# Attention 0: norm factors stored, spread and applied, and outputs stored, each one tile later than the operation it needs

## The chip, the cores and the metric

The kernel runs on one core of a Trainium2 chip. Its time is the device time of one execution in microseconds (us). Five engines of the core matter here: PE (TensorE, matrix products; PEld is its weight load), DVE (VectorE), ACT (ScalarE), POOL (GpSimd) and SP (SyncE, which here only issues transfers). Each engine takes its instructions in the order in which the program has them; an instruction that must wait holds up what stands behind it on the same engine.

## The reference

A two-layer encoder trunk over 1024 positions of width 1024, in 32-bit floats. Layer 0 mixes positions by differential attention with 8 heads, layer 1 by latent attention; each layer has a gate path, an output projection and a residual add. The part that the change touches is the end of a head of layer 0:

```python
def block(qb):
    sc = jnp.einsum('bqhcd,bkhcd->bhcqk', qb, k) * scale
    p = jax.nn.softmax(sc, axis=-1)
    p = p[:, :, 0] - lam * p[:, :, 1]
    return jnp.einsum('bhqk,bkhd->bqhd', p, v)

o = _from_blocks(lax.map(block, _to_blocks(q)))
o = _rmsnorm(o, subln_g) * (1.0 - lambda_init)      # norm over the 128 values of a head
o = o.reshape(b, s, DA_WIDTH) * jax.nn.silu(z)      # gate
return o @ w_out0
```

## The kernel before, in words

Matrix products are made in three passes of a reduced format: each operand is split into a high part (a cast on ACT, to a tile whose name ends in h) and a low part (a subtraction on DVE or POOL, name ending in l). So `woh`, `wol` are the two parts of a weight tile of the output projection, `oah`, `oal` those of an operand tile, and their subtraction is L1199 on both engines. L173 to L175 are the three passes.

Attention 0 runs from about 155 to 685 us. A head takes about 70 us: eight tiles of 128 queries, in two halves of 512. PE makes the scores (L866), DVE and ACT the softmax, PE transposes the probabilities (L395), ACT and DVE split them (`pth` L397, `ptl` L398), and PE multiplies by v. Between these, PE works on the projections of the next heads, for which weights are loaded (`wraw`, L197) and split (`wh` L218 on ACT, `wl` L219 on POOL), and the rotation of q and k (rope, L331 to L370) runs over ACT, SP and POOL: `rp_raw` is copied out, SP swaps its halves into `rp_sw`, POOL multiplies and adds (L336, L341, L343), ACT casts to `qa`, POOL makes the low part `qb` (L366, L367), and SP moves both into place (L369, L370). L1102 to L1123 and L1133 to L1149 combine tiles of the weights and of the outputs for the projection, on POOL, with loads and stores on SP.

At the end of a half, `head_out` brings the output tile `o` out (ACT, L932) with its squares, and `subln` multiplies it by the gate tile `gz` (POOL, L938). The function `rest`, one tile later, sums the squares on PE and gets the norm factors `rq_y` on POOL (L169, L953). These are 512 numbers, 4 in each partition; to multiply `o` with them, each partition needs all 512. So they are stored to memory (`bc_d`, L420) and loaded back spread over all partitions (`bc_s`, L422). Then POOL multiplies (L908), and SP stores the tile to `oF` (L912), where the output projection loads it from. The very last half, (7,1), does not go through memory: its factors are spread by PE (L922).

The order is set so: a list `hooks` holds functions; at the end of each tile's work `after_scores` takes what is in the list at that point and runs it, so that a function which is put into the list by another runs one tile later. `in_turn` keeps the order in which the program is written for POOL, ACT and DVE instructions of this stage; the rest is set by a scheduler by the same writing order. In the last head `rest` is run from a list `rests` by the output projection's own steps (`extra0`), which also load tiles of `oF`: `k11`, `k21`, `k12` and four tiles `ob`. `k12` is the half (7,0); it is loaded right after attention 0 has ended (L1385), and split for the projection.

Of the kernel before, what the change touches and what calls it, by code (L numbers as in the profile page):

```python
# [11 lines left out]
F32 = mybir.dt.float32  # L12
# [9 lines left out]
P = 128  # L22
# [4 lines left out]
HF = 512  # L27
NH = 8
# [48 lines left out]
def f32v(ap):  # L77
    return ap.bitcast(F32)
# [3 lines left out]
def trunk(ctx: ExitStack, tc: tile.TileContext, A, out):  # L82
    nc = tc.nc
    SP, PE, V, S, G = nc.sync, nc.tensor, nc.vector, nc.scalar, nc.gpsimd

    def pool(stack, name, bufs=1, side="left", space=None):
        kw = dict(name=name, bufs=bufs, reuse_waits="tile")
        if space is not None:
            kw["space"] = space
            if space == DRAM:  # L90
                kw.pop("reuse_waits")
        else:
            kw["side"] = side
        return stack.enter_context(tc.tile_pool(**kw))
# [21 lines left out]
    def bank(tag, name, shape=None):  # L116
        nonlocal turn
        if tag == "acc":
            turn += 1
            if (turn - 1) % (2 + NB.get("accx", 0)) < 2:  # L120
                return psa.tile([P, HF], F32, name=name, tag="acc", bufs=2)
            tag = "accx"
        return ps.tile(shape or [P, HF], F32, name=name, tag=tag, bufs=NB[tag])

    dr = pool(ctx, "dr", bufs=1, space=DRAM)
# [6 lines left out]
    oF = [dr.tile([NH, 2, P, HF], F32, name=f"oF{l}") for l in range(2)]  # L132
# [47 lines left out]
    def behind(eng):  # L180

        return tc.issue_after(mk[eng]) if eng in mk else nullcontext()

    def in_turn(ins):

        return tc.keep_in_program_order(ins) if mk else ins
# [230 lines left out]
    def bcast_rows(sp, y, tag, bufs):  # L417

        d_ = dr.tile([HF], F32, name="bc_d", tag="bcd", bufs=4)
        SP.dma_start(d_.rearrange("(p t) -> p t", p=P), y)  # L420
        b = sp.tile([P, HF], F32, name="bc_s", tag=tag, bufs=bufs)
        SP.dma_start(b, d_[None, :].to_broadcast([P, HF]))  # L422
        return b, b.rearrange("p (q t) -> p t q", t=4)

    def t3(ap_):
        return ap_.rearrange("p (t q) -> p t q", t=4)
# [173 lines left out]
    for f in range(2):  # L600
        fs = slice(f * HF, f * HF + HF)
        spread = PE.matmul(cb[:, fs], ones[0:1, :], crow[0:1, fs], start=True, stop=True).ins
# [298 lines left out]

    def finish(o, y, l, h, half, dst, ap_, dgs):

        if dst is None:
            b, rb = bcast_rows(ap_, y, "osq", 4)

            def scale():
                in_turn(G.tensor_mul(t3(o), t3(o), rb))  # L908
                hooks.append(lambda: hooks.append(store))

            def store():
                SP.dma_start(oF[l][h, half], o)  # L912

            if l == 0 and (h, half) >= (NH - 2, 1):
                hooks.append(lambda: hooks.append(scale))
            else:
                hooks.append(scale)
            return
        rb = bank("z", "rb") if l else Y[1]
        for j in range(4):  # L920
            js = slice(j * P, (j + 1) * P)
            S.mul(dgs[:, js], ident, y[:, j : j + 1])  # L922
            PE.matmul(rb[:, js], ones, dgs[:, js], start=True, stop=True)
        V.tensor_mul(o, o, rb)
# [9 lines left out]
    def subln(o, sq, zz, half, h, dst):  # L934


        if dst is None:
            in_turn(G.tensor_mul(o, o, GZ[h][half]))  # L938
        else:
            V.tensor_mul(o, o, GZ[h][half])  # L940

        def rest():
            pt = Y[0] if dst is not None else ssq_at[0] if ssq_at else bank("acc", "ssq")
            for j in range(4):
                PE.matmul(pt[:, j : j + 1], sq[:, j * P : (j + 1) * P], ones[:, 0:1], start=True, stop=True)
            w = sm.tile([P, 4], F32, name="sl_w")
            fin = sm.tile([P, 4], F32, name="sl_f")
            V.tensor_mul(fin, zz, zz)
            V.scalar_tensor_tensor(out=w, in0=fin, scalar=P * EPS / GUARD ** 2, in1=pt[:, 0:4], op0=ALU.mult, op1=ALU.add)
            V.scalar_tensor_tensor(out=fin, in0=fin, scalar=FMAX / GUARD ** 2, in1=w, op0=ALU.mult, op1=ALU.is_ge)  # L950
            V.tensor_scalar(w, w, 3.0e38, None, op0=ALU.min)
            y = rsqrt(w, 4)
            in_turn(G.tensor_mul(y, y, fin))  # L953
            if dst is not None:
                return lambda: finish(o, y, 0, h, half, dst, None, sq)
            finish(o, y, 0, h, half, None, a0b, sq)

        if dst is None:
            (hooks if h < NH - 1 else rests).append(rest)
        else:  # L960
            return rest()
# [29 lines left out]
    tails, hooks = [None, None], []  # L991
# [171 lines left out]
    class Seven:  # L1163
# [32 lines left out]
        def put(self, raw, hi, lo, eng):  # L1196
            with behind("S"):
                S.copy(hi, raw)  # L1198
            sub = eng.tensor_sub(lo, raw, f32v(hi))  # L1199
            if eng is G:  # L1200
                in_turn(sub)
                self.sub = sub.ins
# [871 lines left out]
    def attn1(h, fills, extra=None, late=None):  # L2074
# [5 lines left out]
        def close(half, o_, zz):  # L2080
            if late and half == 1:
                ctx_["late"] = late(o_, zz, ctx_["gz"])
                return
            o = ap2.tile([P, HF], F32, name="o1", tag="o", bufs=2)
            V.scalar_tensor_tensor(out=o, in0=o_, scalar=0.5, in1=ctx_["gz"], op0=ALU.mult, op1=ALU.mult)
            V.reciprocal(zz, zz)
            finish(o, zz, 1, h, half, None, ap2, None)
# [365 lines left out]
```

## Time and profile before

| | us |
|---|---|
| median of the runs (3) | 1396.46 |
| lowest, highest | 1396.01, 1397.87 |
| profiled execution | 1394.95 |
| its span | 1393.2 |
| granted clock of TensorE, mean | 0.999 |
| PE busy | 1367.5 (98%) |
| DVE busy | 928.3 (67%) |
| POOL busy | 753.1 (54%) |
| ACT busy | 740.9 (53%) |

The span is the time from the first to the last instruction that the profile records; all times of instructions are counted from its start. Busy shares are means over the whole span. In rows of the timeline stand start, duration, engine, line, operation, output and inputs, shapes and count, and in brackets the idle time of the engine just before with what ended it. Of the 15 multiplications L908 the first is at 204.74 and the last at 674.75 us.

### The profile page before, as it was taken

How to read it: one execution, taken by the hardware profiler on the slowest of the kernel's cores; microseconds unless marked ns; L12 is line 12 of the kernel's file. 1: busy time of each engine (PE TensorE's matmuls, PEld its weight loads, DVE VectorE, ACT ScalarE, POOL GpSimd, SP SyncE). 2: the span in 40 equal slices, each digit the busy share in tenths (PEclk: the TensorE clock that was granted, in tenths of full speed). 3: DMA queues.
4: the chain of work that ended last, by engine and by line, in shares of the span. 5: the costliest groups of instructions: out<-in, count | busy, mean ns of one | idle time of the engine just before them, and what ended most of it. 6: DMA issues, size and time to landing. Idle time of an engine off the chain costs nothing.

```text
span 1393.2 us, 20695 instructions
## 1 busy us (share of the span) xinstructions
PE 1367.5 (98%) x7334; PEld 1144.7 (82%) x7334; DVE 928.3 (67%) x1313; ACT 740.9 (53%) x1339; POOL 753.1 (54%) x593
## 2 busy tenths in 40 slices
PE   9999999999999999999999999999999999999997
PEld 6788888888888887887887888888888888888886
DVE  7655777777666666668596976545656555555684
ACT  5532465656565555567648553335454544545554
POOL 5424374758686858575794233532141373834673
PEclk9999999999999999999999999999999999999999
DMA  9857644343444434526564246489443364667463
GB/s 342 263 177 244 201 110 141 100 144 105 149 127 144 128 121 122 151 61 212 182 219 167 68 137 212 137 282 286 125 105 119 102 201 136 193 221 215 145 245 121
DMA packets 149386, 232.06 MB, mean 167 GB/s; under 512 B 20641, under 2 KB 57633, under 8 KB 149282
## 3 DMA queue, kind: packets, MB, share of 16 engines
q1 hardware_dynamic: 149282, 230.74, 52.7%
q8 instruction: 58, 0.95, 0.3%
q14 instruction: 46, 0.38, 0.1%
HBM read 144.74 MB, written 61.81 MB: 148 GB/s over the span
## 4 chain that ended last, share of the span: by engine, by line
PE 79%; DVE 6%; DMA 5%; ACT 3%; POOL 3%; issue 2%; SPq 1%; POOLq 0%; ACTq 0%; DVEq 0%
PE s L2067 10%; PE acc L173 9%; PE acc L175 9%; PE acc L174 9%; PE tr L395 7%; PE s L866 7%; PE pv L173 4%; PE pv L174 4%; PE pv L175 4%; PE vps L173 2%; PE vps L174 1%; PE vps L175 1%; PE zacc L175 1%; PE zacc L173 1%; PE zacc L174 1%
## 5 line engine op out<-in xcount | busy, mean ns | idle before, releaser
L397 ACT CAST pth<-tr 128x512 fp32r<-128x512 f32 x256 | 150.3, 587 | 285.7 <-PE tr L395 280.8
L412 DVE TENSOR_REDUCE nm<-s 128x1 f32<-128x1024 f32 x192 | 233.8, 1218 | 79.8 <-PE s L866 70.9
L398 DVE TENSOR_TENSOR ptl<-tr,pth 128x512 fp32r<-128x512 f32 x256 | 176.1, 688 | 150.3 <-ACT pth L397 146.3
L219 POOL TENSOR_TENSOR wl<-wraw,wh 128x512 fp32r<-128x512 f32 (+2 forms) x77 | 98.8, 1284 | 208.4 <-ACT wh L218 176.3
L414 ACT ACTIVATE e<-s,nm 128x1024 f32<-128x1024 f32 x128 | 143.5, 1121 | 35.4 <-DVE nm L412 35.0
L395 PE MATMUL tr<-ident,e 128*128 128x128 f32 x1024 | 155.0, 273 | 4.1 <-DVE ptl L398 3.8
L395 PEld LDWEIGHTS tr<-ident,e 128*128 128x128 f32 x1024 | 120.7, 140 | 46.5 <-DVE ptl L398 24.1
L173 PE MATMUL acc<-h0h,wh 128*128 128x512 f32 x360 | 150.2, 417 | 0.0
L173 PE MATMUL pv<-pth,vt 128*128 128x256 f32 x512 | 147.5, 288 | 0.0
L174 PE MATMUL pv<-ptl,vt 128*128 128x256 f32 x512 | 145.6, 284 | 0.0
L175 PE MATMUL pv<-pth,vt 128*128 128x256 f32 x512 | 144.6, 282 | 0.0
L175 PE MATMUL acc<-h0h,wl 128*128 128x512 f32 x360 | 141.5, 393 | 0.0
L174 PE MATMUL acc<-h0l,wh 128*128 128x512 f32 x360 | 141.1, 392 | 0.0
L336 POOL TENSOR_TENSOR rp_r<-rp_raw,cosT 128x512 f32<-128x512 f32 x36 | 47.0, 1305 | 104.4 <-ACT rp_raw L333 52.9
L173 PEld LDWEIGHTS pv<-pth,vt 128*128 128x128 f32 x512 | 97.2, 190 | 2.9 <-ACT pth L397 0.2
L174 PEld LDWEIGHTS pv<-ptl,vt 128*128 128x128 f32 x512 | 97.4, 190 | 2.4
L175 PEld LDWEIGHTS pv<-pth,vt 128*128 128x128 f32 x512 | 97.3, 190 | 0.0
L1199 POOL TENSOR_TENSOR wol<-wol,woh 128x512 fp32r<-128x512 f32 x56 | 82.3, 1492 | 26.0 <-ACT woh L1198 24.4
L866 PE MATMUL s<-ks,qa 128*128 128x512 f32 x256 | 82.7, 403 | 4.4 <-DVE e L874 3.2
L874 DVE SCALAR_TENSOR_TENSOR e<-s,z,e 128x1024 f32<-128x1024 f32 x64 | 82.2, 1284 | 2.2
L866 PE MATMUL s<-ks,qb 128*128 128x512 f32 x256 | 79.8, 393 | 1.2 <-DMA qb<-qb 1.2
L175 PEld LDWEIGHTS acc<-h0h,wl 128*128 128x128 f32 x360 | 67.6, 188 | 15.1
(427 smaller groups left out, 3461.1 us busy)
## 6 DMA issues: line engine op xcount, KB each, us to landing
ada<-in_ada_ss SPq DMA_DIRECT2D x32, 512.0 KB, 5.9
wraw<-in_w_s SPq DMA_DIRECT2D x64, 256.0 KB, 2.8
vS<-v_hl SPq DMA_DIRECT2D x32, 512.0 KB, 5.9
vt<-vS SPq DMA_DIRECT2D x32, 512.0 KB, 4.9
wol<-tS SPq DMA_DIRECT2D x56, 256.0 KB, 5.2
tS<-ob SPq DMA_DIRECT2D x48, 256.0 KB, 2.0
rp_sw<-rp_raw SPq DMA_DIRECT2D x160, 64.0 KB, 2.0
bc_s<-bc_d SPq DMA_DIRECT2D x34, 256.0 KB, 4.2
```

Of the source, the lines that this page charges most:

```text
L173: PE.matmul(psum, ah, bh, start=first, stop=False, skip_group_check=skip)
L174: PE.matmul(psum, ah, bl, start=False, stop=False, skip_group_check=skip)
L175: mm3.last = PE.matmul(psum, al, bh, start=False, stop=last, skip_group_check=skip).ins
L219: sub = (V if pair_of else G).tensor_sub(l_[:, :n], raw[:, :n], f32v(h_[:, :n]))
L395: transpose_p.last = PE.transpose(tr[:, j, :], p[:, kt * P : (kt + 1) * P], ident).ins
L397: mk["S"] = S.copy(pth[kh][:, :, dst], tr).ins
L398: mk["V"] = V.tensor_sub(ptl[kh][:, :, dst], tr, f32v(pth[kh][:, :, dst])).ins
L412: mk["V"] = V.reduce_max(nm, s_ps, axis=AX.X, negate=True).ins
L414: mk["S"] = S.activation(e, s_ps, AF.Exp, bias=nm, scale=1.0, accum_out=zs).ins
L866: PE.matmul(s_ps[:, kc * HF : (kc + 1) * HF], src[:, c, ql], KS[h][kc][:, c, :], start=fst, stop=not fst)
L1199: sub = eng.tensor_sub(lo, raw, f32v(hi))
L2067: PE.matmul(s_ps[:, kc * HF : (kc + 1) * HF], lhs, rhs(kc), start=i == 0, stop=i == 4)
```

## The change

For layer 0, `finish` becomes a chain of four hooks. Before, the factors were stored and loaded back at once where they had been made, the multiplication ran one tile later (two for the halves (6,1) and (7,0)), and the store of the output two tiles after it. Now each of store of factors, spread load, multiplication and store of the output is a hook put into the list by the one before: one, two, three and four tiles after the factors. Layer 1 keeps its order. No instruction is added or removed; lines behind `finish` have numbers higher by 20, so L1199 is L1219, L938 is L958, and L908, L912, L420, L422 are L919, L923, L909, L914 for layer 0.

```diff
     def finish(o, y, l, h, half, dst, ap_, dgs):
 
+        if dst is None and l == 0:
+            d_ = dr.tile([HF], F32, name="bc_d", tag="bcd", bufs=4)
+            rb = []
+
+            def put():
+                SP.dma_start(d_.rearrange("(p t) -> p t", p=P), y)
+                hooks.append(spread)
+
+            def spread():
+                b = ap_.tile([P, HF], F32, name="bc_s", tag="osq", bufs=4)
+                SP.dma_start(b, d_[None, :].to_broadcast([P, HF]))
+                rb.append(b.rearrange("p (q t) -> p t q", t=4))
+                hooks.append(scale)
+
+            def scale():
+                in_turn(G.tensor_mul(t3(o), t3(o), rb[0]))
+                hooks.append(store)
+
+            def store():
+                SP.dma_start(oF[l][h, half], o)
+
+            hooks.append(put)
+            return
         if dst is None:
             b, rb = bcast_rows(ap_, y, "osq", 4)
...
-            if l == 0 and (h, half) >= (NH - 2, 1):
-                hooks.append(lambda: hooks.append(scale))
-            else:
-                hooks.append(scale)
+            hooks.append(scale)
             return
```

Where this moves instructions is shown at three places. The first is POOL in head 4: the multiplication of the half (3,1) by its factors, and the gate of the half (4,0). Before:

```order
L343 TENSOR_TENSOR rp_r<-rp_r,rp_sw 128x512
L219 TENSOR_TENSOR wl<-wraw,wh 128x512
L908 TENSOR_TENSOR o<-o,bc_s 128x512
L1112 TENSOR_TENSOR ob_4305<-ob_4305,c_202 128x512 x2
L358 TENSOR_TENSOR ks<-rp_r,ks 64x512
L359 TENSOR_TENSOR ks<-rp_r,ks 64x512
L336 TENSOR_TENSOR rp_r<-rp_raw,cosT 128x512
L341 TENSOR_TENSOR rp_sw<-rp_sw,sinT 128x512
```

Ten rows of POOL later, and in the changed kernel at the same place:

```order
L336 TENSOR_TENSOR rp_r<-rp_raw,cosT 128x512
L358 TENSOR_TENSOR ks<-rp_r,ks 64x512
L359 TENSOR_TENSOR ks<-rp_r,ks 64x512
L219 TENSOR_TENSOR wl<-wraw,wh 128x512
L958 TENSOR_TENSOR o<-o,gz 128x512
L919 TENSOR_TENSOR o<-o,bc_s 128x512
L1142 TENSOR_TENSOR ob_4303<-ot_4670,ob_4303 128x512
L1143 TENSOR_TENSOR ob_4304<-ob_4304,ot_4670 128x512
L341 TENSOR_TENSOR rp_sw<-rp_sw,sinT 128x512
L343 TENSOR_TENSOR rp_r<-rp_r,rp_sw 128x512
```

The multiplication by the factors has moved from behind a weight split to right behind the gate of the next half; the rest of the order is the same. It is the same move for the other halves before (7,0).

The second place is POOL at the end of attention 0: the multiplication of the half (7,0), the splits for the output projection, the split of the tile `k` that is loaded from this half's store, and the factors of the last half. Before:

```order
L1199 TENSOR_TENSOR wol<-wol,woh 128x512
L908 TENSOR_TENSOR o<-o,bc_s 128x512
L1199 TENSOR_TENSOR oal<-oal,oah 128x512
L1199 TENSOR_TENSOR wol<-wol,woh 128x512 x2
L1199 TENSOR_TENSOR oal<-k_6673,oah 128x512
L1145 TENSOR_TENSOR ob<-ob 128x512
L1146 TENSOR_TENSOR ob<-ob 128x512
L1148 TENSOR_TENSOR ob<-ob 128x512
L1149 TENSOR_TENSOR ob<-ob 128x512
L169 TENSOR_TENSOR rq_y<-sl_w,mhalf 128x4
```

And in the changed kernel:

```order
L1219 TENSOR_TENSOR wol<-wol,woh 128x512
L1219 TENSOR_TENSOR oal<-oal,oah 128x512
L1219 TENSOR_TENSOR wol<-wol,woh 128x512 x2
L919 TENSOR_TENSOR o<-o,bc_s 128x512
L1219 TENSOR_TENSOR oal<-k_6670,oah 128x512
L1165 TENSOR_TENSOR ob<-ob 128x512
L1166 TENSOR_TENSOR ob<-ob 128x512
L1168 TENSOR_TENSOR ob<-ob 128x512
L1169 TENSOR_TENSOR ob<-ob 128x512
L169 TENSOR_TENSOR rq_y<-sl_w,mhalf 128x4
```

The multiplication has moved behind three splits and stands directly ahead of the split of `k`, its own product loaded back.

The third place is SP's queue there (`tS`, `sS` and `oF` are in memory; a load of `k` or `ob` reads stored outputs). Before:

```order
L1355 DMA ob<-oF_81 128x512 x4
L1179 DMA wol<-tS_83 128x512
L1179 DMA oal<-oF_81 128x512
L1179 DMA wol<-tS_83 128x512
L1179 DMA oal<-oF_81 128x512
L420 DMA bc_d<-rq_y 128x4
L422 DMA bc_s<-bc_d 128x512
L1179 DMA wol<-tS_83 128x512
L1179 DMA oal<-oF_81 128x512
L1179 DMA wol<-tS_83 128x512
L912 DMA oF_81<-o 128x512
L1385 DMA k_6673<-oF_81 128x512
```

And in the changed kernel:

```order
L1199 DMA wol<-tS_83 128x512
L923 DMA oF_81<-o 128x512
L909 DMA bc_d<-rq_y 128x4
L1372 DMA k_6669<-oF_81 128x512
L1375 DMA ob<-oF_81 128x512 x4
L914 DMA bc_s<-bc_d 128x512
L923 DMA oF_81<-o 128x512
L1405 DMA k_6670<-oF_81 128x512
L1199 DMA wol<-tS_83 128x512 x4
L1199 DMA oal<-sS_85 128x512 x2
```

All loads of `wol` and `oal` that stood between now stand ahead, the store of the half (6,1) and the loads of `ob` come behind them, and the spread load of the last factors stands directly ahead of the store that it leads to.

## The prediction

> **What bounds the kernel now.** I read the page's head first, then the waits of PE by the stage that the change touches (140 to 700 us), then the engines' own timelines there.
>
> ```profile
> span 1393.2 us, 20695 instructions
> PE 1367.5 (98%) x7334; PEld 1144.7 (82%) x7334; DVE 928.3 (67%) x1313; ACT 740.9 (53%) x1339; POOL 753.1 (54%) x593
> PE s L866 <- DVE e L874: 3.2, 6, 1.0
> PE tr L395 <- DVE ptl L398: 2.8, 5, 0.9
> ```
>
> PE is busy 1367.5 of 1393.2 us, so all its idle time is 25.7 us. In attention 0 the largest idle groups (sum, count, longest) are 3.2 and 2.8 us. The change adds and removes no instruction, so the time moves only where one of PE's waits vanishes, grows or appears. I therefore follow each moved operation until a PE instruction waits for what stands behind it, or until an idle gap absorbs it.
>
> What moves is small. For each of 15 output tiles (head, half), one multiplication by the spread norm factors (L908, about 1.55 us on POOL) moves later in POOL's order, and three transfers move later in SP's. In the new order each L908 stands right behind the gate multiplication L938 of the next half. Both queues run in order; the outputs stay the same tiles and sizes, so no transfer gets longer by itself. Whatever stood behind the old place can run earlier by up to 1.55 us plus any wait for the factors, and what stands behind the new place runs 1.55 us later, unless idle time there takes it.
>
> **The change, part by part.** In heads 0 to 2 POOL has idle time between either place and its next consumer, and PE's few waits there are for other things; I cost them at nothing. Heads 3 to 6 are tighter.
>
> Head 3 gains:
>
> ```profile
> 376.25 1.55 POOL L908 TENSOR_TENSOR o<-o,bc_s 128x512 f32<-128x512 f32 x1 [1.83 <-DMA bc_s<-bc_d]
> 386.35 1.29 POOL L341 TENSOR_TENSOR rp_sw<-rp_sw,sinT 128x512 f32<-128x512 f32 x1 [1.95 <-DMA rp_sw<-rp_raw]
> 391.87 0.69 ACT L932 ACTIVATE o<-pv,g 128x512 f32<-128x512 f32 x1
> 396.81 1.29 POOL L938 TENSOR_TENSOR o<-o,gz 128x512 f32<-128x512 f32 x1
> 403.27 1.29 POOL L219 TENSOR_TENSOR wl<-wraw,wh 128x512 fp32r<-128x512 f32 x1
> 409.96 0.70 PE L866 MATMUL s<-ks,qa 128*128 128x512 f32 x2 [0.88 <-DMA qa<-qa]
> 411.22 0.70 PE L866 MATMUL s<-ks,qb 128*128 128x512 f32 x2 [0.55 <-DMA qb<-qb]
> ```
>
> Each row is start, duration, engine, line, operands and, in brackets, the idle time ahead with what ended it. The old L908 cost 1.83 idle plus 1.55 busy, up to 3.4 us, and the swap transfer of rope behind it is issued earlier, so the 1.95 at 386.35 need not return. L938 can go at 392.56 + the queue, about 393.4 (o is ready at 391.87 + 0.69), against 396.81: 3.4 earlier. The moved L908 then takes 1.55 back: 1.85 net at L219 (403.27), whose input buffer the next weight load of SP waits for, with the qa and qb copies queued behind it. PE's two waits are 0.88 and 0.55, both under 1.85, so both go: **-1.4**.
>
> Heads 4 and 6 lose:
>
> ```profile
> 446.39 1.54 POOL L908 TENSOR_TENSOR o<-o,bc_s 128x512 f32<-128x512 f32 x1
> 450.99 2.41 SPq L335 DMA_DIRECT2D rp_sw<-rp_raw  x4
> 454.95 1.29 POOL L341 TENSOR_TENSOR rp_sw<-rp_sw,sinT 128x512 f32<-128x512 f32 x1 [0.43 <-DMA rp_sw<-rp_raw]
> 465.53 1.30 POOL L938 TENSOR_TENSOR o<-o,gz 128x512 f32<-128x512 f32 x1
> 471.96 0.62 ACT L364 CAST qa<-rp_r 64x512 fp32r<-64x512 f32 x1 [2.23 <-POOL rp_r L343]
> 475.10 0.66 PE L395 MATMUL tr<-ident,e 128*128 128x128 f32 x4 [0.87 <-DVE ptl L398]
> 603.24 1.28 POOL L938 TENSOR_TENSOR o<-o,gz 128x512 f32<-128x512 f32 x1 [4.07 <-ACT o L932]
> 612.51 0.62 ACT L364 CAST qa<-rp_r 64x512 fp32r<-64x512 f32 x1 [2.28 <-POOL rp_r L343]
> 615.16 0.66 PE L395 MATMUL tr<-ident,e 128*128 128x128 f32 x4 [0.40 <-DVE ptl L398]
> ```
>
> In head 4 the old L908 (446.39) goes, but L341 at 454.95 still waits for a transfer that SP issues at 450.99, so its 1.54 us come back as idle. From 454.95 POOL runs without a gap through L938 at 465.53, and the L908 put behind that makes rope's last step 1.55 later. ACT waits for that step already (2.23), in order, ahead of the probability splits that PE waits for at 475.10 (0.87 now). Nothing between has slack, so the wait grows by the whole: **+1.5**. Head 6 is the same: L938 at 603.24 has 4.07 idle before it, so nothing done earlier helps, and ACT's 2.28 and PE's 0.40 each grow by 1.55: **+1.5**. In head 5 ACT also waits for rope, by
>
> ```profile
> 541.99 0.62 ACT L364 CAST qa<-rp_r 64x512 fp32r<-64x512 f32 x1 [1.60 <-POOL rp_r L343]
> 551.32 0.70 PE L866 MATMUL s<-ks,qb 128*128 128x512 f32 x2 [0.66 <-DMA qb<-qb]
> ```
>
> and its cast comes later by between nothing and 1.55, by how much of the time that the old L908 frees survives until then (POOL has no gap in between, but its inputs come from SP and ACT at their own times); I take 0.95, past the middle towards the late end, as head 4 gave back nothing; but the spread load, which was issued ahead of the qb copies that PE waits 0.66 for, now stands behind them. I set the two against each other: **0**, with ends -0.7 and +1.0.
>
> The junction with the output projection carries the largest term. The half (7,0) is stored and loaded back as an operand (k) of that projection:
>
> ```profile
> 674.75 1.57 POOL L908 TENSOR_TENSOR o<-o,bc_s 128x512 f32<-128x512 f32 x1
> 677.51 2.53 POOL L1199 TENSOR_TENSOR wol<-wol,woh 128x512 fp32r<-128x512 f32 x2
> 677.18 0.64 ACT L1198 CAST woh<-wol 128x512 fp32r<-128x512 f32 x1
> 682.06 1.29 POOL L1199 TENSOR_TENSOR oal<-k,oah 128x512 fp32r<-128x512 f32 x1 [2.02 <-ACT oah L1198]
> 683.31 1.29 POOL L1145 TENSOR_TENSOR ob<-ob 128x512 f32<-128x512 f32 x1
> 687.41 1.60 POOL L1149 TENSOR_TENSOR ob<-ob 128x512 f32<-128x512 f32 x1
> 689.32 1.02 POOL L169 TENSOR_TENSOR rq_y<-sl_w,mhalf 128x4 f32<-128x4 f32 x1 [0.30 <-DVE sl_w L951]
> 676.34 0.32 SPq L912 DMA_DIRECT2D oF<-o  x1
> 678.40 0.32 SPq L1385 DMA_DIRECT2D k<-oF  x1
> 678.77 1.85 SPq L1179 DMA_DIRECT2D wol<-tS  x4
> k<-oF SPq DMA_DIRECT2D x1, 256.0 KB, 2.7
> 690.65 1.28 ACT L922 ACTIVATE sq<-ident,rq_y 128x128 f32<-128x128 f32 x4 [4.42 <-POOL rq_y L953]
> ```
>
> L908 moves from 674.75 to behind three L1199 splits. The last two took 2.53 together from 677.51; with L908 out of their way all three come 1.5 earlier, except that the last can't start before ACT's cast of its operand ends (677.18 + 0.64 = 677.82). It ends at 679.1 (half of 2.53 later), so L908 runs from 679.1 to 680.65, 4.35 later than before. Then, step by step: the store is issued at 680.7; the load 2.06 later (678.40 less 676.34), at 682.7; it lands 2.7 later, at 685.5; cast to 686.1; the split oal<-k at 686.15 against 682.06; the four multiplications L1145 to L1149, queued behind it, take 5.7 and end at 693.1; then rq_y, the norm factor of the last half, against 689.32. It is 3.8 late. ACT's scaling, which already waits 4.42 for it, and then DVE follow:
>
> ```profile
> 692.48 1.29 DVE L1199 TENSOR_TENSOR oal<-oal,oah 128x512 fp32r<-128x512 f32 x2 [3.23 <-ACT oah L1198]
> 693.69 0.68 DVE L1199 TENSOR_TENSOR oal<-ob,oah 128x512 fp32r<-128x512 f32 x1
> 695.50 0.69 DVE L1420 TENSOR_TENSOR x<-x,oz 128x512 f32<-128x512 f32 x1 [0.53 <-PE oz L175]
> 707.86 1.78 DVE L1199 TENSOR_TENSOR oal<-ob,oah 128x512 fp32r<-128x512 f32 x1
> 710.00:720.00 10.00, 10.00 (x45) 8.26 (x44) 10.00 (x11) 3.89 (x8) 10.00 (x7) 1.00 0.35 127
> 726.90 0.50 PE L173 MATMUL oz<-woh,oah 128*128 128x512 f32 x1 [0.37 <-DVE x L1420]
> ```
>
> DVE's run starts at 692.48, has one gap of 0.53 (695.50) and then none: the window row gives, from the third number, busy time of PE, PEld, DVE, ACT and POOL, and DVE and POOL are busy all ten us. So 3.8 - 0.5 = 3.3 stay in it until PE waits for it at 726.90, with 0.37 of idle already, that is with no slack left. **+3.3**. Its ends: 0 if PE's wait is really set by something not delayed (PE could then run ahead), and 4.35 if the 0.53 gap does not absorb.
>
> Here a rule speaks against my 3.3. The row first: the same DVE subtraction took 0.68 at 693.69, when POOL was idle, and 1.78 at 707.86 beside a busy POOL. The Trainium skill, "SBUF — State Buffer", section "Who interferes with whom", says that a DVE instruction with two SBUF inputs and a GpSimd instruction that reads SBUF exclude each other, one fully blocking the other. These two rows agree. By that rule the shift of 3.8 on POOL against 3.3 on DVE changes which operations meet, by 0.5 us, which could free or hit one subtraction: 1.1 either way, so the sum would be 3.8 or 6.0 instead of 4.9.
>
> On SP four loads of wol stand behind the load of k; they were issued from 678.77 and now go from about 683.1. At the 2.7 that k took, or even twice that, they land by 690, ahead of DVE's and POOL's work on them, which starts after rq_y: 0, and up to +1 if the transfers bunch. One queue thing helps: the operand loads that stood behind (7,0)'s factor store on SP now stand ahead of it.
>
> Elsewhere SP's stores and loads issued later only find more room: in heads 0 to 2 the transfers they pass have no PE wait behind them. In head 7 before the junction POOL's idle time for the factors of (6,1) goes, but the casts on ACT, whose order hardly changes, set what follows: 0, at best -0.5.
>
> **The sum**: -1.4 + 1.5 + 0 + 1.5 + 3.3 = +4.9. The profiled execution took 1394.95 us (span 1393.2 and 1.75 around it), 1.51 under the median of the runs shown. Against it: 1399.85; on the median, 1396.46 + 4.9 = **1401.4**.
>
> **Rivals.**
> - *The junction absorbs.* PE's wait at 726.90 is only 0.37, and a PE that waits for DVE there might be given the time back at the end of the projection, or the split oal<-k may be overtaken in effect by faster transfers (SP's queue is emptier). Then only -1.4 + 1.5 + 1.5 = +1.6 stays: 1398.1. For it: PE has other idle time in the projection. Against it: DVE and POOL both full in 710 to 720.
> - *Larger loss.* The gain in head 3 fails, because L938 is held by POOL work that depends on other transfers, and the same late step costs its 1.55 there: +4.9 + 1.4 + 1.5 = +7.8; with head 5's +1.0 it is 1405.2. Against it: the 1.83 of idle at 376.25 is plainly lost to the spread load.
> - *Faster.* Taking transfers that POOL waits for out of its way is all that matters, and L908 finds cover wherever it stands. This is decided in the junction: from the point where k's split is ready by 682.06 after all, nothing is late. Then PE's waits 0.88, 0.55 and 0.66 go and head 7 gives 0.5 to 0.8: -2.8, 1393.6. Against it: the wait of 2.02 at 682.06 shows that k is already the last to arrive before the L908 moves 4.35 later.
> - *The change does nothing measurable*: the reordering is real in heads 4 and 6, but every cost is absorbed: 1396.5. It lies in the first rival's side of the range.
>
> **How the numbers follow.** The likeliest is the sum, 1401.4, with 0.56; its own range is 1399.3 to 1403.5 (the rule's 1.1, and one of the 1.5 terms out). The junction absorbed or all absorbed: 0.27. Larger loss: 0.10. Faster: 0.07. A measurement of this kernel tells about 0.2% (2.8 us) from no change: 1393.7 to 1399.3 counts as same. So slower is 0.56 + 0.10 = 0.66, same 0.27, faster 0.07. The range of 8 in 10 leaves out the faster case and the far end of the large loss, and takes in absorption: 1396.0 to 1405.0.
>
> **What would show it.** In the changed kernel: PE's waits at 410 for qa and qb gone; the waits of transposes for DVE's ptl near 475 and 615 above 1.5; the (7,0) scale near 679, the split of k near 686, rq_y near 693, DVE's run from about 696; PE idle in 699 to 735 of some 3 us more in all. The forecast is wrong if k lands before 683, if DVE's run shows gaps in 700 to 735, or if POOL has idle time between the moved L908 and rope in heads 4 and 6.

## The result and the profile after

The changed kernel takes 1404.2 us (median of 6 runs, 1403.39 to 1404.7) against 1396.36 (6 runs, 1394.79 to 1397.87) of the kernel before: a ratio of 1.0055, 95% interval [1.0042, 1.0068], so 5.9 to 9.5 us slower. The forecast was 1401.4 with 1396.0 to 1405.0: the direction and the range hold, and the loss of 7.8 us is 1.6 times the 4.9 forecast. The profiled execution has a span of 1401.5 us.

The head of its page, and the largest groups of PE's waits in the same window as before (sum, count, longest):

```profile
span 1401.5 us, 20683 instructions
PE 1369.4 (98%) x7334; PEld 1144.2 (82%) x7334; DVE 931.9 (66%) x1313; ACT 741.1 (53%) x1339; POOL 757.5 (54%) x593
PE s L866 <- DVE e L874: 4.8, 5, 1.2
PE tr L395 <- DVE ptl L398: 4.7, 7, 1.1
PE oy L175 <- POOL oal L1219: 1.1, 2, 0.6
PE oy L173 <- ACT oah L1218: 1.1, 1, 1.1
PE oy L174 <- POOL wol L1219: 1.0, 1, 1.0
```

PE's busy time hardly moved (1367.5 to 1369.4); what grew is waiting. The two groups that led before grew by 1.6 and 1.9, three at the junction are new or larger, and the waits for the copies of qa and qb near 410 are gone. The places, in the timelines of the changed kernel, head 3 first:

```profile
393.76 1.30 POOL L958 TENSOR_TENSOR o<-o,gz 128x512 f32<-128x512 f32 x1
395.02 1.56 POOL L919 TENSOR_TENSOR o<-o,bc_s 128x512 f32<-128x512 f32 x1
471.98 0.62 ACT L364 CAST qa<-rp_r 64x512 fp32r<-64x512 f32 x1 [3.78 <-POOL rp_r L343]
472.18 0.74 PE L866 MATMUL s<-ks,qa 128*128 128x512 f32 x2 [1.15 <-DVE e L874]
475.12 0.66 PE L395 MATMUL tr<-ident,e 128*128 128x128 f32 x4 [1.05 <-DVE ptl L398]
483.44 1.30 POOL L341 TENSOR_TENSOR rp_sw<-rp_sw,sinT 128x512 f32<-128x512 f32 x1 [5.03 <-DMA rp_sw<-rp_raw]
544.80 0.62 ACT L364 CAST qa<-rp_r 64x512 fp32r<-64x512 f32 x1 [2.58 <-POOL rp_r L343]
547.94 0.66 PE L395 MATMUL tr<-ident,e 128*128 128x128 f32 x4 [0.89 <-DVE ptl L398]
615.59 0.62 ACT L364 CAST qa<-rp_r 64x512 fp32r<-64x512 f32 x1 [3.78 <-POOL rp_r L343]
615.77 0.74 PE L866 MATMUL s<-ks,qa 128*128 128x512 f32 x2 [1.15 <-DVE e L874]
626.40 1.29 POOL L341 TENSOR_TENSOR rp_sw<-rp_sw,sinT 128x512 f32<-128x512 f32 x1 [4.38 <-DMA rp_sw<-rp_raw]
```

Head 3's gate comes at 393.76 (396.81 before). ACT's wait for rope in heads 4 and 6 grew from 2.23 and 2.28 to 3.78, by the 1.5 of the moved multiplication, and PE waits twice for what comes after: 1.15 for DVE's `e`, where it had no wait before, and then 1.05 (head 4) and 0.57 (head 6, at 618.24) for `ptl`. Two rows stand for something that the prediction lacks: POOL waits 5.03 and 4.38 for the second rope's swap transfers (3.30 and 3.22 before). And the junction:

```profile
670.88 0.50 PE L174 MATMUL oy<-wol,oah 128*128 128x512 f32 x1 [0.95 <-POOL wol L1219]
682.90 1.55 POOL L919 TENSOR_TENSOR o<-o,bc_s 128x512 f32<-128x512 f32 x1
689.84 1.28 POOL L1219 TENSOR_TENSOR oal<-k,oah 128x512 fp32r<-128x512 f32 x1 [5.39 <-ACT oah L1218]
689.82 0.50 PE L173 MATMUL oy<-woh,oah 128*128 128x512 f32 x1 [1.13 <-ACT oah L1218]
691.17 0.50 PE L175 MATMUL oy<-woh,oal 128*128 128x512 f32 x1 [0.63 <-POOL oal L1219]
696.86 1.01 POOL L169 TENSOR_TENSOR rq_y<-sl_w,mhalf 128x4 f32<-128x4 f32 x1
700.01 1.29 DVE L1219 TENSOR_TENSOR oal<-oal,oah 128x512 fp32r<-128x512 f32 x2 [4.26 <-ACT oah L1218]
734.40 0.50 PE L173 MATMUL oz<-woh,oah 128*128 128x512 f32 x1 [0.37 <-DVE x L1440]
```

The kernel enters this stage 3.8 us late. Taking that off, the multiplication of (7,0) is at 679.1, k's split at 686.0, the last factors at 693.1, DVE's run at 696.2: the forecast's four times (679.1, 686.15, 693.1, 696.3) within 0.2. DVE's gap of 0.53, which was to take 0.5 off this, shrank to 0.1, but a split just behind it (first the kernel before, then the changed one) took 0.43 longer, and the rest of the run is 3.8 late:

```profile
696.71 1.00 DVE L1199 TENSOR_TENSOR oal<-oal,oah 128x512 fp32r<-128x512 f32 x1
703.81 1.42 DVE L1219 TENSOR_TENSOR oal<-oal,oah 128x512 fp32r<-128x512 f32 x1
```

### The profile page after: what moved, and what is told of

Same layout as the page of the kernel before. It is cut to its first block, busy times and chain, and to the rows that moved or that the text cites. A ratio compares the mean times of both kernels' runs of the same rounds, so it can differ in the third digit from the quotient of the medians.

```text
span 1401.5 us, 20683 instructions
## 1 busy us (share of the span) xinstructions
PE 1369.4 (98%) x7334; PEld 1144.2 (82%) x7334; DVE 931.9 (66%) x1313; ACT 741.1 (53%) x1339; POOL 757.5 (54%) x593
## 4 chain that ended last, share of the span: by engine, by line
PE 81%; DVE 6%; DMA 4%; POOL 3%; ACT 3%; issue 2%; SPq 1%; POOLq 0%; ACTq 0%; DVEq 0%
PE s L2087 10%; PE acc L173 9%; PE acc L175 9%; PE acc L174 9%; PE tr L395 7%; PE s L866 7%; PE pv L173 4%; PE pv L175 4%; PE pv L174 4%; PE vps L173 2%; PE vps L174 2%; PE vps L175 2%; PE zacc L175 1%; PE zacc L174 1%; PE zacc L173 1%
## 5 line engine op out<-in xcount | busy, mean ns | idle before, releaser
L219 POOL TENSOR_TENSOR wl<-wraw,wh 128x512 fp32r<-128x512 f32 (+2 forms) x77 | 102.0, 1326 | 219.4 <-ACT wh L218 174.5
L1219 POOL TENSOR_TENSOR wol<-wol,woh 128x512 fp32r<-128x512 f32 x56 | 82.3, 1492 | 28.1 <-ACT woh L1218 25.6
```

The source lines that it names most:

```text
L219: sub = (V if pair_of else G).tensor_sub(l_[:, :n], raw[:, :n], f32v(h_[:, :n]))
```

## The experiments

All are made from the changed kernel: its chain of hooks is replaced by a table that gives for each half how many tiles after its factors were made they are stored, spread, multiplied and the output stored. With the changed kernel's delays it gives the changed kernel's order on every engine (e9's trace); with the delays of before and one half late, the orders on POOL and SP in the traces of e1, e3, e4 and e7 differ from the kernel before only around that half.

```diff
+LATE_ALL = (0, 0, 1, 3)
+LATE = {(6, 1): (0, 0, 2, 4), (7, 0): (0, 0, 2, 4)}    # the kernel before
...
+            steps = [put, spread, scale, store]
+            at = LATE.get((h, half), LATE_ALL)
+
+            def run(n):
+                while steps and at[4 - len(steps)] <= n:
+                    steps.pop(0)()
+                if steps:
+                    hooks.append(lambda: run(n + 1))
+
+            run(0)
```

The changed kernel is `(1, 2, 3, 4)` for all. Lines of the attention loop stand 2 lower down in these kernels, L938 and the ones behind `finish` 28.

Two measures follow for each. The ratio is of runs beside runs of the kernel before on the same chip. The steps are from one trace each: how much later than in the profiled execution of before the same DVE instructions start (median over a stretch of time), less the same in the stretch before. The first 200 us, the same in all kernels, differed by 0.0 to +2.9 from one execution to the next; the steps leave that out, the ratios don't. A step is good to about 0.1. Heads 0 to 2, which the table leaves out, moved by -0.4 to +0.2. Nor is one wait for ACT near 757 in the steps: it is 0.99 in the changed kernel's first trace, 0.46 in that of before and 0.45 in e9.

| run | ratio [95%] | head 3 | head 4 | head 5 | head 6, first rope | head 6, second rope | junction |
|---|---|---|---|---|---|---|---|
| changed kernel | 1.0055 [1.0042, 1.0068] | -1.4 | +3.3 | -0.2 | +1.5 | +0.6 | +3.9 |
| e9, changed again | 1.0056 [1.0043, 1.0068] | -1.5 | +2.1 | -0.3 | +1.5 | +1.0 | +3.9 |
| e1, (3,1) late | 1.0011 [1.0002, 1.0019] | -0.2 | +2.1 | -1.0 | 0.0 | 0.0 | 0.0 |
| e2, (3,1) on POOL | 1.0010 [1.0002, 1.0019] | 0.0 | +1.5 | -0.9 | 0.0 | 0.0 | -0.1 |
| e3, (2,1) late | 0.9987 [0.9979, 0.9996] | -1.7 | 0.0 | -1.0 | 0.0 | 0.0 | 0.0 |
| e4, (7,0) late | 1.0031 [1.0019, 1.0043] | -0.2 | 0.0 | -1.1 | 0.0 | 0.0 | +3.5 |
| e5, three undone | 1.0016 [1.0008, 1.0025] | -1.5 | +0.1 | -0.3 | 0.0 | +0.6 | +4.1 |
| e6, factors early | 1.0070 [1.0057, 1.0082] | -1.5 | +1.5 | +0.1 | +1.5 | 0.0 | +7.8 |
| e7, (5,1) late | 1.0008 [1.0000, 1.0017] | -0.3 | 0.0 | -1.1 | +1.5 | 0.0 | 0.0 |
| e8, (7,0) undone | 1.0053 [1.0039, 1.0067] | -1.5 | +1.6 | -0.2 | +1.5 | +0.9 | +3.4 |
| e10, (6,1) undone | 1.0050 [1.0037, 1.0063] | -1.4 | +1.5 | -0.3 | +1.5 | +1.3 | +3.2 |
| e11, both undone | 1.0021 [1.0012, 1.0030] | -1.5 | +2.2 | -0.2 | +1.5 | +1.2 | +0.1 |
| e12, late to (3,0) | 0.9993 [0.9984, 1.0001] | -1.4 | 0.0 | -0.2 | 0.0 | 0.0 | +0.2 |

**Head 4.** e1 has `(3, 1): (1, 2, 3, 4)`, e2 has `(3, 1): (0, 0, 2, 4)`, added to the table of before.

> The kernel before, with the new delays (factors stored one tile, spread two, multiplied three, stored four tiles after they are made) for the half (3,1) alone, so that only head 4 changes. Theory P (the multiplication in a gapless run of POOL is the whole cost): +1.5 us, all of it in PE's wait for transposes near 475; nothing more after it. Theory T (the reordering on SP's queue adds its own cost: a weight load now stands ahead of the copies of qa and holds them until POOL frees its buffer, and the swap transfers of the second rope land later): +3.2 us, of which 1.5 by 476 and 1.7 between 478 and 492.

> The kernel before, with the half (3,1) multiplied one tile later instead of three: POOL gets the multiplication inside the same gapless run ahead of rope's last step, while SP's queue around the copies of qa keeps the order of before. Theory P: +1.5 us, the same as the run with the full delays of (3,1). Theory T: +1.5 us here, against +3.2 there; the swap transfers of the second rope land as in the kernel before, and POOL waits 3.3 us for them, not 5.0. If neither holds and POOL's place costs nothing: 0.

By the clock both cost the same, 0.3 to 2.7 us; the traces part them. PE's waits and POOL's wait for the second rope, in e1 (first four rows) and in e2:

```profile
476.70 0.73 PE L868 MATMUL s<-ks,qa 128*128 128x512 f32 x2 [1.11 <-DVE e L876]
479.64 0.66 PE L397 MATMUL tr<-ident,e 128*128 128x128 f32 x4 [1.04 <-DVE ptl L400]
485.26 0.70 PE L868 MATMUL s<-ks,qb 128*128 128x512 f32 x2 [0.24 <-DMA qb<-qb]
486.83 1.28 POOL L343 TENSOR_TENSOR rp_sw<-rp_sw,sinT 128x512 f32<-128x512 f32 x1 [3.92 <-DMA rp_sw<-rp_raw]
```

```profile
473.77 0.73 PE L868 MATMUL s<-ks,qa 128*128 128x512 f32 x2 [1.11 <-DVE e L876]
476.71 0.66 PE L397 MATMUL tr<-ident,e 128*128 128x128 f32 x4 [1.06 <-DVE ptl L400]
483.25 1.28 POOL L343 TENSOR_TENSOR rp_sw<-rp_sw,sinT 128x512 f32<-128x512 f32 x1 [3.26 <-DMA rp_sw<-rp_raw]
```

The first two waits are the same: 2.15 and 2.17, less 0.87 that was there before. So POOL's part is 1.5, as theory P says. What theory T adds is there too, but unsteady. SP's queue in the kernel before (first rows) and in the changed one:

```profile
473.64 0.50 SPq L369 DMA_DIRECT2D qa<-qa  x1
474.45 0.33 SPq L197 DMA_DIRECT2D wraw<-in_w_s  x1
474.83 0.50 SPq L370 DMA_DIRECT2D qa<-qa  x1
```

```profile
474.47 0.33 SPq L197 DMA_DIRECT2D wraw<-in_w_s  x1
474.89 0.50 SPq L369 DMA_DIRECT2D qa<-qa  x1
475.44 0.59 SPq L370 DMA_DIRECT2D qa<-qa  x1
```

In both the weight load goes out when POOL's split of the tile in its buffer has ended, at 474.4. With the order of before (qa's first copy ahead of the weight load), POOL's wait for the second rope was 3.26 to 3.30 in all seven traces that have it. With the weight load ahead, which holds both copies until then, seven traces show 3.26, 3.30, 3.40, 3.87, 3.92, 4.03 and 5.03, and head 4's step in the same seven is 1.5, 1.5, 1.6, 2.1, 2.1, 2.2 and 3.3: what the swap transfers land later, PE loses. So four of seven are late with the new order and none of seven with the old; why three of seven are not is open. The mean of this part is 0.6, not the 1.7 of the one trace that I had gone by.

**Head 3.** e3 adds `(2, 1): (1, 2, 3, 4)`.

> The kernel before, with the new delays for the half (2,1) alone, so that only head 3 changes. The prediction's step for head 3: PE's waits of 0.88 and 0.55 us for qa and qb near 410 go, -1.4 us, and nothing comes back in head 4 (since the multiplication of (3,1) stays where it was): 1395.0. Rival: the gain is eaten in head 4, because POOL there waits for rope's transfers at a time that PE sets, and PE has caught up with it: -0.3 to 0.

In its timeline PE has no wait worth listing between 336 and 474 any more; -1.7 in the trace, and -0.6 to -2.9 by the clock. Nothing comes back in head 4. The step is -1.5 in e6 as well (below), where the factors are stored and spread at once: it comes from the later multiplication or the later store of the output, not from the transfers of the factors. e12 (the first seven halves late) was to carry this over to a version better than both:

> The kernel before with the new delays for the first seven halves, (0,0) to (3,0), except that all later ones keep the old timing: a version meant to beat both kernels. If heads 0 to 2 absorb the moves, as the prediction has it: the time of (2,1) alone, 1.5 to 2 us below the kernel before. If not, the sum is lost in heads 0 to 2 or by (3,0) in head 4: 0 or above.

It measured 1394.53 against 1395.13, a ratio that is not clear of 1; its trace shows the same -1.4 in head 3 and nothing lost in heads 0 to 2. The kernel with (2,1) alone remains the fastest measured, 1393.51 against 1395.61, and the only one faster than both by more than its interval.

**Head 6.** e7 adds `(5, 1): (1, 2, 3, 4)`.

> The kernel before, with the new delays for the half (5,1) alone, so that only head 6 changes. The prediction's step: +1.5 us, in PE's wait near 615. With the second stage that the trace of the changed kernel shows (the swap transfers of the second rope land 1.2 later, because weight loads are no longer held behind the output's store and go beside them): +2.0.

The first stage is there and steady, +1.5 in every trace with (5,1) late (e7 by the clock: 0.0 to 2.4). The second isn't: e7's POOL waits 3.40 for the second rope, as before. It needs the lateness of (6,0), whose factors are spread in that stretch: in e5 (below) (6,0) is late and (5,1) is not, and POOL waits 4.43. e6 asks which part of that lateness it is (`LATE_ALL = (0, 0, 3, 4)`, factors stored and spread at once):

> All 15 halves with the factors stored and spread at once, as in the kernel before, and the multiplication and the store of the output as late as in the changed kernel. Theory P (it is the place of the multiplication that costs, not that of the factors' transfers): the time of the changed kernel, +7.8 us, within 1. Theory T (the transfers of the factors, one and two tiles later, collide with the rope's swaps and the operand loads): 1.5 to 3 us less than the changed kernel, since the collisions of the spread load in heads 4 and 6 and at the junction are gone.

POOL's wait for the second rope in e6, and in e9 (the changed kernel's order):

```profile
625.65 1.29 POOL L343 TENSOR_TENSOR rp_sw<-rp_sw,sinT 128x512 f32<-128x512 f32 x1 [3.29 <-DMA rp_sw<-rp_raw]
```

```profile
627.12 1.28 POOL L343 TENSOR_TENSOR rp_sw<-rp_sw,sinT 128x512 f32<-128x512 f32 x1 [4.86 <-DMA rp_sw<-rp_raw]
632.45 0.66 PE L397 MATMUL tr<-ident,e 128*128 128x128 f32 x4 [0.81 <-DVE ptl L400]
```

SP's queue shows what differs. In the changed kernel (first rows) the spread load goes out right behind the swap transfers, and weight loads with it, since the output's store that held them back before (last rows, kernel before) has moved away:

```profile
621.23 2.45 SPq L335 DMA_DIRECT2D rp_sw<-rp_raw  x4
623.73 0.58 SPq L914 DMA_DIRECT2D bc_s<-bc_d  x1
624.40 1.05 SPq L1199 DMA_DIRECT2D wol<-tS  x1
```

```profile
616.79 0.54 SPq L422 DMA_DIRECT2D bc_s<-bc_d  x1
618.15 2.44 SPq L335 DMA_DIRECT2D rp_sw<-rp_raw  x4
626.36 0.33 SPq L912 DMA_DIRECT2D oF<-o  x1
626.79 0.38 SPq L1179 DMA_DIRECT2D wol<-tS  x1
```

In e6 neither goes out beside the swaps: the spread load stands ahead of them, and the weight load is issued at 632.75. So a late transfer costs 0.6 to 1.3 us here, as theory T has it, but which of the two loads does it, or both, was not separated. As a whole e6 went against theory T: it is no faster than the changed kernel. Theory P's +7.8 within 1 can't be told from its +8.0 to +11.4 by the clock, but its trace is not the changed kernel's, since it loses 7.8 at the junction. There its last operand loads stand behind the loads of `ob`, in the order of e5, below, and the multiplication of (7,0) is late as well.

**The junction.** e4 adds `(7, 0): (1, 2, 3, 4)` to the table of before; e8 takes it out of the changed kernel; e5 gives (3,1), (5,1) and (7,0) back.

> The kernel before, with the new delays for the half (7,0) alone, so that only the junction with the output projection changes. The prediction's step: the split of k about 4 us later, the factors of the last half 3.8 later, DVE's run 3.8 later, +3.3 us in all, with the 0.53 gap of DVE taking the rest. Rival 1 (the junction absorbs): 0 to +1. Rival 2 (the gap absorbs nothing and splits and loads behind it bunch as well): +3.8 to +4.8, some of it after 735.

> The changed kernel with the half (7,0) given back its old timing. If the junction's cost adds to the rest: 4.4 us less than the changed kernel, as the single run of (7,0) showed, +3.4 against the kernel before, and PE's waits at 690 to 735 as in the kernel before. If the junction also suffers from what (6,1) does there: less is given back, +4 to +5.

> The changed kernel with the three halves whose delay was found or forecast to cost, (3,1), (5,1) and (7,0), given back their old timing; the other twelve keep the new delays. If the three places (and head 3's gain from (2,1)) are the whole of the change: the time of the run with (2,1) alone, about 2 us below the kernel before, 1393.5. If the other eleven halves cost something too (singles so far: +1.6 for (3,1), -2.1 for (2,1), +4.4 for (7,0); the whole change +7.8, so up to 4 us is not found yet, of which (5,1) was forecast to hold 1.5 and the trace shows 2.0): 1394.5 to 1396.

Alone, the lateness of (7,0) costs what the prediction worked out: 3.5 in the trace, 2.7 to 6.0 by the clock. But taking it out of the changed kernel gave next to nothing (+7.4 remains, where +3.4 or +4 to +5 was expected), a miss, and e5 was 1.7 us slower than before where I had expected it faster. PE and ACT at the junction in e5:

```profile
666.54 0.50 PE L176 MATMUL oy<-wol,oah 128*128 128x512 f32 x1 [0.95 <-POOL wol L1227]
676.72 0.66 PE L397 MATMUL tr<-ident,e 128*128 128x128 f32 x4 [1.12 <-DVE ptl L400]
678.65 0.50 PE L175 MATMUL oy<-woh,oah 128*128 128x512 f32 x1 [1.28 <-ACT p L1314]
676.98 0.62 ACT L1226 CAST oah<-oal 128x512 fp32r<-128x512 f32 x1 [2.29 <-DMA oal<-oF]
```

ACT waits 2.29 us for an operand load, with casts that PE needs queued behind it (in e8 1.63, at 680.49). SP's queue there in e5, and the loads of `ob` in the kernel before:

```profile
668.12 2.03 SPq L1383 DMA_DIRECT2D ob<-oF  x3
670.53 0.32 SPq L915 DMA_DIRECT2D bc_s<-bc_d  x1
671.37 0.42 SPq L1207 DMA_DIRECT2D oal<-oF  x1
```

```profile
652.94 2.29 SPq L1355 DMA_DIRECT2D ob<-oF  x4
```

These four loads of 256 KB stand behind the store of (6,1) in SP's queue (one reads what it writes). With (6,1) late they move from 653 to between 665 and 670, directly ahead of that operand load. The changed kernel has the operand loads ahead of them (issued by 657, the loads of `ob` from 674), and pays for (7,0) instead; with (7,0) undone, the order turns and the price is paid here. Two ways to lose about the same, of which the changed kernel takes one. e6 takes both: ACT waits 1.48 for the operand load and then 3.97 for k, and the step is 7.8. Then undoing both must give it back:

> The changed kernel with the half (6,1) given back its old timing, (7,0) still late. If the part of the junction's cost that the prediction lacked (4.5 in the trace against 3.3) is the multiplication of (6,1) in POOL's run ahead of a split that PE waits for (0.95 at 671): 1.2 us less than the changed kernel, and that wait is gone. If it is something else: the same time as the changed kernel.

> The changed kernel with both (6,1) and (7,0) given back their old timing, so that the junction has the order of before on SP and POOL. If the junction holds 4.5 us of the change, and undoing (7,0) alone gave little because (6,1)'s late store still pushed 1 MB of operand loads ahead of the spread load and of the last operand loads: 4.5 less than the changed kernel, about +2.5 to +3 against the kernel before, with PE's waits at 664 to 760 as there. If undoing both gives no more than (7,0) alone: +5 or more.

e11 does: its junction step is 0.1, and the ratio falls from 1.0056 (e9, on the same chip) to 1.0021. With (6,1) alone undone PE's wait of 0.95 near 671 is gone, and 0.7 less is lost at the junction than in e9; e10's expectation of 1.2 was too much, and the two ratios can't tell it from nothing.

> The changed kernel once more, its delays written as a table, with the same instructions in the same order on every engine: the total on the chip and beside the runs of the kernel before with which the other three are compared, and a second trace. +7 to +8 us. If the second stage in head 4 (1.3 us of PE's waits at 480 to 489, after swap transfers that landed 1.7 later) is a property of the new order, it is in this trace as well; if it belongs to the one execution, as the runs e6 and e8, which have the same order there and don't show it, suggest, PE waits only 0.7 there and the trace is shorter by about 1.

The repetition gives +7.8 us again. PE's waits from 480 to 490 are 0.34 here against 1.29 in the first trace: the size belongs to the execution.

## Why the prediction came out as it did

- *Head 3, -1.4*: -1.4 to -1.7 in nine traces. Right, by its own steps; the gate at 393.76 was forecast at 393.4.
- *Head 4, +1.5*: 1.5 for POOL's part, right, though PE lost it in two waits (1.15 and 1.05) and not in one above 1.5. What failed is the sentence that SP's transfers issued later only find more room: the move reordered SP's queue, and swap transfers landed later in four of seven traces, for 0.6 more on the mean.
- *Head 5, 0*: failed. ACT's wait grew by 0.98 (1.60 to 2.58; 0.95 was estimated), but the gain set against it, PE's wait of 0.66 for qb, was no property of the kernel before: five other traces with head 5 in its old order don't have it, and so stand at -0.9 to -1.1 in the table (a sixth, e12, has it with 0.58, and stands at -0.2; in it and in the trace of before POOL waits 4.11 and 4.27 for the second rope's swaps, in the five 3.22 to 3.28). Against those five, the seven traces with new delays in head 5 are at -0.3 to +0.1: a cost of 0.8.
- *Head 6, +1.5*: 1.5 in seven traces, right; the second rope's 0.6 to 1.3 (mean of six 0.9) is missing from the sum, by the same sentence on transfers issued later.
- *Junction, +3.3*: 3.2 and 3.5 where (7,0) is late and (6,1) isn't, 3.9 in the changed kernel. The step for (7,0) is right to 0.2 us in its times, and DVE's run is as late as forecast. Two things in it were wrong. PE did not lose it all in 699 to 735: it lost 2.3 by 692, around its waits at 689.82 and 691.17 for k's own split, and 1.5 behind DVE's run. And the gap of 0.53 took nothing off. The term left (6,1) at zero. Where it is late and (7,0) isn't, the junction costs 3.4 and 4.1; that the changed kernel does not pay this as well, as e6 does, is luck in the total: the prediction names the order behind it (the operand loads now stand ahead) but puts no price on it.
- *The sum*: -1.4 + 1.5 + 0.6 + 0.8 + 1.5 + 0.9 + 3.9 = 7.8, as measured. What the forecast lacked, 2.9, is 0.8 from head 5, 1.5 from transfers moved on SP in heads 4 and 6, and 0.6 from the junction. The terms are means over different traces, and the clock gives 5.9 to 9.5: that the two sums meet to a tenth is luck.
- *The rivals*: the junction absorbed nothing, and so the change was not without effect either. The larger loss comes nearest in time (1405.2), but of its steps only head 5's came (0.8 of 1.0): head 3's gain did not fail. *Faster* was decided in the junction as it said, against it. The rule of the Trainium skill ("SBUF — State Buffer", section "Who interferes with whom") would have moved the sum by 1.1 either way; one subtraction in DVE's run took 0.43 longer, in the changed kernel and in e4, beside a busy POOL in both kernels. No run here separates that rule from another cause.

## What to carry to other kernels

An operation that was moved later out of a queue's wait gained here only where the queue caught up before someone waited for it (head 3); in a run without gaps it cost its full duration, and this could be read off the timeline to a tenth of a us (heads 4 and 6). Read the order of the DMA queue as closely as that of the engines: a store that moves also stops holding back, or starts holding back, the loads behind it, and a load released early can land on top of a transfer that is waited for. A single wait of half a us in one trace is not yet a property of the kernel, and two late steps in one chain need not add, so undoing one of them may show nothing: undo both before calling either harmless.

## What was not expected of the hardware

In head 4 the same order on SP's queue gave arrival times of the same swap transfers that differed by 1.8 us between traces (POOL's wait 3.26 to 5.03), while the order without a weight load ahead of the copies kept them within 0.04 (3.26 to 3.30). In head 5 the order of before alone gave both, 3.22 to 3.28 in five traces and 4.11 and 4.27 in two. So the order on SP does not decide it by itself; what else does, no run here shows.
